# Retention and gMLP on one core: new order of SBUF slots, a later decay table, two weight sums by DMA

## The chip, the cores and the metric

The kernel runs on one core of one Trainium2 chip. The metric is device time in microseconds (us), from one launch to its end. Three runs of the kernel before are at hand; a fourth execution was recorded by the hardware profiler, and its span is the time from the first to the last instruction of the program.

## The reference

Two layers act on 512 latent tokens x and 256 context tokens ctx, 1024 wide, all in float32:

```python
h  = rmsnorm(x, g) * (1 + scale) + shift            # scale, shift, gate from c @ ada_w
# layer 0, bidirectional retention, 4 heads (q, k 256 wide; v, z 512 wide)
q, k, v, z = h @ w_in                                # q and k of latent tokens get axial rope
o  = sum over both directions of (q k^T * decay) v   # latent reads context + latent
x  = x + gate * ((o / rms(o)) * silu(z)) @ w_out
# layer 1, gMLP
u, v, z = h @ w_in                                   # each 2048 wide
v  = layernorm(v) * vnorm_g
y  = u * (w_s @ v + b_s) * silu(z)                   # w_s mixes 128 tokens, 8 groups
x  = x + gate * (y @ w_out)
return rmsnorm(x, final_g)
```

## The kernel before, in words

**Numbers in halves.** TensorE multiplies float32 operands in its fp32r form. So that the product keeps float32 accuracy, each operand is split in two: a high half, which ScalarE (ACT) makes by a cast, and a low half, which VectorE (DVE) makes as source minus high half (`split`, line 132). `mm3` (126) multiplies two operands by three matmuls: low by high, high by low, high by high. Each matmul first loads its stationary operand (128 columns, on the engine PEld of the profile) and then streams its moving operand (256 or 512 columns). The load for the next matmul runs while the present one streams.

**Products.** The matrices are cut in quarters, and a product of quarters by Strassen and Winograd's scheme takes seven products of sums in place of eight: B11, T1, T2, B21, T3, B22, T4 (`Product`, 435; `SINGLE`, 153; in pairs of weights `PAIRED`, 152). One such product is 24 matmuls of 256 columns. In `tokens` (425) the activations are stationary and the weights move; in `features` (396) and `outward` (415) the weights are stationary and the activations move. `WITH` (151) says which sum of activations (A11, A12, A22, S1 to S4) meets which sum of weights.

**Weights.** `Stream` (155) loads raw quarters into 4 KB slots (`pump`), makes the weights' sums T1 to T4 in place, and splits each into one of four `hl` slots (`upto`, two products ahead of use). T1 and T2 are sums on DVE (`sum`, 241). T3, and T4 of the weights `wo` and `o2`, are sums that the GpSimd queue (POOL) makes by an accumulating DMA from one raw slot onto another (`add`, 179; `by_queue`, 189).

**Order.** The order of the products is written out by hand. Within it, the framework's scheduler orders the instructions of each engine by readiness, save where a `Queue` (38) keeps or pins the order of the text; `bound` (1066) pins what it runs behind the instruction before it. The stages, with their place in the profile: layer 0's scores of modulation and first projection (to 56 us), the other projections (to 327), retention of heads 0 and 1 (`attend_two`, to 380), their output projection (`out_two`, to 419), head 2 (`attend_one`, 1344, and `project_out`, 1469, to 468), head 3 (to 522), gMLP's v (to 600), its u and z in eight quads `u` 0 to 7 (1898; to 820), with the output projection of the first half of y as the pair `o2` behind u 3 (`out_pair`, 1755; 685 to 725) and of the rest in `out1` (1782; from 788, and from 820 to the end).

**Retention.** `attend` (1244) makes scores for a pair of key blocks (`score`), on DVE multiplies them with the decay table into `pf`, splits them into `ph` (ACT) and `pl` (DVE), and two steps later multiplies them with v (`pv`, 512 columns). `decay` (1086) makes a head's tables by exponentials on ACT: first those of the latent keys, then those of the context keys (`ct`), then it loads Sqrt's table again. It is a generator: `plan` and `works` say behind which product its next piece is run. For head 2 all three pieces stand ahead of `attend_one` (1501 to 1503).

**gMLP.** For each quad u the normalized v is loaded into slot w7 (`load_vt`), normalized by four ACT instructions (`norm_vt`, 1857), and mixed by `spatial` in the middle of B22, the sixth product of the quad.

**Slots.** All of SBUF is laid out by hand: the `lay` lines (90 to 107) allot the slots one after another, each rounded up to 32 bytes. Counted modulo 256 bytes, the slots oA11 to oS4, hc, s1, w4, w5 and g3 begin at 0; s0, s2, s3, rope, w6, g2, w0 to w3, w7, g0, g1 and dec at 64; the t2 slots at 192. A weight in an `hl` slot begins at 64 where it is stationary and at 192 where it moves (`hl_tile`, 110). The first four weights of gMLP's v do not go there but into oS1, oS2, oA22 and oS3 (`hl_e`, 329 and 347), at 0. The operands `ye` of `o2` are two separate 4 KB halves (`halved_y`, 1712); the low half lies in g3 or s1 (at 0) for A11, S1, S4 and A22, and in s3 or g1 (at 64) for A12, S2 and S3.

```python
def hl_tile(moves=False):
    i = hls[0] % HL
    hls[0] += 1
    t = st([P, 2080], f"hl{i}", F32R, name="hl")
    o = 32 if moves != (i % 2 == 1) else 0
    return t[:, o:o + 2048].rearrange("p (a n) -> p a n", a=2)
```

Of the kernel before, what the change touches and what calls it, by code (L numbers as in the profile page):

```python
# [13 lines left out]
P = 128  # L14
# [53 lines left out]
def hybrid_kernel(ctx, tc, xT_d, cT_d, cv_d, sv_d, rows_d, ada0_d, adag_d, w_d, rope_d, dec_d, ws_d, id_d, out_d):  # L68
# [17 lines left out]
    HL = 4  # L86
# [7 lines left out]
    lay({"ones": 512, "sv": 448, "ident": 512, "eps": 4, "cpad": 1024, "root": 4, "lg": 32, "gs0": 64, "sh0": 64,  # L94
         "sq0": 16, "sq1": 16, "sq2": 16, "rs0": 1024, "rs1": 1024, "rs2": 1024, "shb": 16, "gate0": 32, "gs1": 32,
         "sh1": 32, "shs": 16, "la": 32, "lb": 32, "lc": 32, "sum0": 16, "sum1": 16, "bns": 256, "mv": 32, "rv": 16})
# [3 lines left out]
    lay({"oA11": 8192, "oA12": 8192, "oA22": 8192, "oS1": 8192, "oS2": 8192, "oS3": 8192, "oS4": 8192, "hc": 16384,  # L100
         "s1": 4096, "w4": 4096, "w5": 4096, "g3": 4096, "cv": 64})

    lay({"s0": 4096, "s2": 4096, "s3": 4096, "rope": 4096, "w6": 4096, "g2": 4096, "hl0": 8576})

    lay({"t2": 2048}, T2)
    lay({"hl1": 8320, "hl2": 8576, "hl3": 8320})
# [3 lines left out]
    def hl_tile(moves=False):  # L110

        i = hls[0] % HL
        hls[0] += 1
        t = st([P, 2080], f"hl{i}", F32R, name="hl")
        o = 32 if moves != (i % 2 == 1) else 0
        return t[:, o:o + 2048].rearrange("p (a n) -> p a n", a=2)
# [38 lines left out]
    class Stream:  # L155
# [23 lines left out]
        def add(self, must=None):  # L179

            for e in list(self.due):
                key, tick, to, src = e
                q = key[0]
                if (q, src) in self.raws and (key == must or self.tick > tick):
                    self.due.remove(e)
                    self.added.add(key)
                    nc.gpsimd.dma_start(self.raws[q, to], self.raws[q, src], accum_op=ALU.add)  # L187
# [53 lines left out]
        def sum(self, n):  # L241
# [17 lines left out]
            if name == "T2" and q[0] in ("wo", "o2"):  # L259
                self.due.append(((q, "T4"), self.tick, "21", "11"))  # L260
# [102 lines left out]
    for i in range(UZ):  # L363
# [3 lines left out]
        if i == 3:  # L367
# [3 lines left out]
            for u in ("11", "21", "12", "22"):  # L371
                for q in OUT1:
                    Q.load((q, u), W + ["w7"], 3, parts_of(q, u))
# [8 lines left out]
    def op(key):  # L382
        A[key] = st([P, 2, 4, HS], "o" + key, F32R)
# [378 lines left out]
    def come(*what, then=None):  # L762
# [3 lines left out]
        for kb, th in what:  # L766
# [4 lines left out]
            else:  # L771
                name = NAMES[th][g]
                if k == 0:
                    A[name] = st([P, 2, 4, HS], AT_S3.get(name, "o" + name), F32R)
# [311 lines left out]
    def decay(h, tags=None):  # L1086
# [60 lines left out]
    def load_wo(h):  # L1147
        raws = []
        for c in range(4):
# [5 lines left out]
            w = hl_tile()  # L1155
# [6 lines left out]
    def v_tile(h, tag):  # L1162

        if h != 1:
            return st([P, 2, 2, 512], tag, F32R, name="v")
        i = hls[0] % HL
        hls[0] += 1
        o = 16 if i % 2 else 48
        t = st([P, 2048 + o], f"hl{i}", F32R, name="v")
        return t[:, o:].rearrange("p (a b n) -> p a b n", a=2, b=2)  # L1170
# [173 lines left out]
    def attend_one(h, qs, vs, wo, steps, own=()):  # L1344

        og = [st([P, 2, 4, HS], tag, F32R, name="og") for tag in ("oS3", "oS4")]
# [9 lines left out]
        for i in range(2):  # L1356
            plan[i, 2] += [of(work) for work in own]
        return og, attend((h,), plan, turn)

    def attend_two(qs, vs, ds, q2):  # L1360
# [4 lines left out]
        def operand(key):  # L1365
            t = A[key] = st([P, 2, 4, HS], ROOM[key], F32R)
# [102 lines left out]
    def project_out(ws, og, flip, parts, then=None, between=None, prepare=None):  # L1469
        for hf in range(2):  # L1470
            sl = slice(hf * HS, hf * HS + HS)
            for c in range(4):
# [9 lines left out]
                for mi in range(2):  # L1482
# [25 lines left out]
    for work in own:  # L1508
        drained(work)
# [224 lines left out]
    def y_sums():  # L1734
        v = st([P, 4, HS], "g0", name="yv")
        dve.tensor_tensor(v, y22, y21, ALU.subtract)
        halved_y("S1", v, "g2", "g3")
# [9 lines left out]
        halved_y("S4", y12, "g2", "g3")  # L1747
# [4 lines left out]
        halved_y("A22", y22, "g2", "g3")  # L1752
        yield

    def out_pair():
# [3 lines left out]
        for name in PAIRED:  # L1759
            for q in OUT1:  # L1760
# [10 lines left out]
                n += 1  # L1771
        gb = Q.gate = st([P, D], "g1", name="gb")
        load(gb, gate_d.partition_broadcast(P))
        late_rows["fg"] = fg = st([P, D], "g0", name="fg")
        load(fg, rows_d[1:2, :].partition_broadcast(P))
        ya = st([P, 4, 2, SEQ], "hc", F32R, name="ya")
        ys.extend([ya[:, i] for i in range(4)] + [st([P, 2, SEQ], f"g{i}", F32R, name="yb") for i in (2, 3)])
# [120 lines left out]
    for i in range(UZ):  # L1898
        got, pms = {}, {}
        prod = Product(features, got.__setitem__)  # L1900
        for name in SINGLE:
# [5 lines left out]
            if name == "T2":  # L1907
                norm_vt(i)
# [4 lines left out]
            if name == "B22":  # L1913
# [5 lines left out]
                if i == 3:  # L1919
                    Q.free.append("w7")  # L1920
# [5 lines left out]
            if (i, name) == (2, "B21"):  # L1926
                halved_y("A11", y11, "s0", "s1")
# [3 lines left out]
        if i == 3:  # L1931
            out_pair()
            Q.free.remove("w7")
# [115 lines left out]
```

## Time and profile before

| | before |
|---|---|
| runs | 865.73, 863.9, 865.46 us; median 865.46 |
| profiled execution | 861.68 us |
| its span | 859.8 us (1.9 us lie around it) |
| granted TensorE clock in the span | 0.998 |
| busy in the span | PE 850.1, PEld 821.2, DVE 723.8, ACT 487.8, POOL 88.9 us |
| matmuls | 6966 |

A row of the timeline gives the start, the duration, the engine, the operation, output and inputs, and the count of instructions merged into it; the bracket behind it is the engine's idle time just before and what ended it. A matmul's duration reaches past the start of the next one, because matmuls are pipelined. The pitch, the time from one start to the next, is therefore taken between the starts of two rows, divided by the count. In a row of the groups by shape the columns behind the bar are busy time, mean duration of one in ns, and idle time before.

### The profile page before, as it was taken

To read this page: it belongs to the slowest core of one execution; us is meant where nothing else is said; L and a number is where in the kernel's file an instruction comes from. 1 tells how busy PE (TensorE), PEld (TensorE's weight loads), DVE (VectorE), ACT (ScalarE), POOL (GpSimd) and SP (SyncE) were. 2 spreads that over 40 slices of the span, in tenths; PEclk is the share of its full clock that TensorE was granted. 3 is DMA by queue.
4 is the path that set the end of the run, shared out by engine and by line. 5 is a ranking of instruction groups with operands and counts; after the bars stand their busy time and mean duration, and the time that the engine had idled before them with its cause. 6 is when DMAs were issued, how large, how long until landed. Compare 5 with 4: busy or idle time off the path is not lost.

```text
span 859.8 us, 17428 instructions
## 1 busy us (share of the span) xinstructions
PE 850.1 (99%) x6966; PEld 821.2 (96%) x6966; DVE 723.8 (84%) x1015; ACT 487.8 (57%) x770; POOL 88.9 (10%) x132
## 2 busy tenths in 40 slices
PE   9999999999999999999999999999999999999996
PEld 7899999999999999899989899999999999999985
DVE  4799899869977985799687879998888998788895
ACT  4566644455365355567873559754656665565434
POOL 0001211211211011000001012121000010000110
PEclk9999999999999999999999999999999999999999
DMA  9945857876977797257486943547555557546532
GB/s 358 406 131 154 245 175 255 261 216 183 311 218 226 221 305 264 75 123 219 162 273 186 261 113 111 197 135 244 173 148 144 152 129 215 154 141 197 123 49 99
DMA packets 82049, 166.70 MB, mean 194 GB/s; under 512 B 8624, under 2 KB 39728, under 8 KB 81968
## 3 DMA queue, kind: packets, MB, share of 16 engines
q1 hardware_dynamic: 68592, 122.90, 43.4%
q0 software_dynamic: 12944, 42.48, 20.1%
q8 instruction: 55, 0.90, 0.4%
q10 hardware_dynamic: 432, 0.20, 0.1%
q14 instruction: 26, 0.21, 0.1%
HBM read 125.17 MB, written 24.12 MB: 174 GB/s over the span
## 4 chain that ended last, share of the span: by engine, by line
PE 94%; ACT 3%; DMA 1%; DVE 1%; issue 1%; ACTq 0%; DVEq 0%
PE pst L54 94%; DMA vt<-vt 1%; DMA ident<-in_id_dram 1%; ACT acc L54 0%; DVE o L54 0%; ACT L54 0%; ACT junk L54 0%; ACT hl L54 0%; ACT dt L54 0%; ACT vt L54 0%; ACT qk L54 0%; DVE snap L54 0%; ACT de L54 0%; DVE ada_h L54 0%; DVE v L54 0%
## 5 line engine op out<-in xcount | busy, mean ns | idle before, releaser
L54 DVE TENSOR_TENSOR hl<-raw,hl 128x1024 fp32r<-128x1024 f32 (+2 forms) x209 | 249.7, 1200 | 56.4 <-ACT hl L54 55.9
L54 ACT CAST hl<-raw 128x1024 fp32r<-128x1024 f32 (+2 forms) x209 | 214.4, 1031 | 128.6 <-DVE raw L54 61.9
L54 PE MATMUL pst<-oS,hl 128*128 128x256 f32 x1296 | 155.2, 277 | 0.1
L54 PEld LDWEIGHTS pst<-oS,hl 128*128 128x128 f32 x1296 | 150.6, 188 | 1.2 <-issue 0.8
L54 PE MATMUL pst<-hl,oS 128*128 128x256 f32 x1152 | 134.7, 276 | 0.0
L54 PE MATMUL pst<-oA,hl 128*128 128x256 f32 x1080 | 133.9, 279 | 0.1
L54 PEld LDWEIGHTS pst<-hl,oS 128*128 128x128 f32 x1152 | 132.4, 188 | 0.8 <-issue 0.4
L54 PEld LDWEIGHTS pst<-oA,hl 128*128 128x128 f32 x1080 | 127.3, 188 | 1.8 <-issue 0.4
L54 DVE TENSOR_TENSOR raw<-raw 128x1024 f32<-128x1024 f32 x77 | 93.9, 1220 | 0.9
L54 PE MATMUL pst<-hl,oA 128*128 128x256 f32 x768 | 92.1, 277 | 0.0
L54 ACT ACTIVATE snap<-pst 128x512 f32<-128x512 f32 x87 | 51.7, 594 | 68.0 <-PE pst L54 67.9
L54 PEld LDWEIGHTS pst<-hl,oA 128*128 128x128 f32 x768 | 89.3, 188 | 0.0
L54 PE MATMUL pst<-v,ph 128*128 128x512 f32 x192 | 59.8, 393 | 0.0
L187 POOL DMA_DIRECT2D raw<-raw x31 | 27.0, 870 | 278.8 <-DVE raw L54 166.9
L54 DVE TENSOR_TENSOR snap<-snap,pst 128x512 f32<-128x512 f32 x75 | 51.0, 680 | 3.0 <-PE pst L54 2.9
L54 PE MATMUL pst<-og,hl 128*128 128x256 f32 x384 | 46.3, 280 | 0.0
L54 PEld LDWEIGHTS pst<-og,hl 128*128 128x128 f32 x384 | 45.0, 188 | 0.2
L54 PEld LDWEIGHTS pst<-v,ph 128*128 128x128 f32 x192 | 36.1, 188 | 7.0
L54 PE MATMUL pst<-hl,ye 128*128 128x256 f32 x336 | 40.4, 282 | 0.0
L54 PEld LDWEIGHTS pst<-hl,ye 128*128 128x128 f32 x336 | 40.1, 188 | 0.1
L54 PE MATMUL pst<-v,pl 128*128 128x512 f32 x96 | 37.8, 394 | 0.9 <-DVE pl L54 0.9
L54 ACT CAST ph<-pf 128x512 fp32r<-128x512 f32 x24 | 14.9, 621 | 40.2 <-DVE pf L54 40.2
(240 smaller groups left out, 1134.9 us busy)
## 6 DMA issues: line engine op xcount, KB each, us to landing
raw<-in_w_dram SPq DMA_DIRECT2D x208, 256.0 KB, 3.9
bg<-in_adag_dram SPq DMA_DIRECT2D x32, 512.0 KB, 5.1
raw<-raw POOLq DMA_DIRECT2D x31, 512.0 KB, 5.4
ada_w<-in_ada_dram SPq DMA_DIRECT2D x16, 512.0 KB, 8.5
raw<-in_w_dram SPq DMA_DIRECT2D x16, 512.0 KB, 4.5
v<-snap POOLq DMA_DIRECT2D x16, 256.0 KB, 4.6
z<-snap POOLq DMA_DIRECT2D x16, 256.0 KB, 4.5
v<-v SPq DMA_DIRECT2D x8, 512.0 KB, 6.7
```

Of the source, the lines that this page charges most:

```text
L54: made = op(*args, **kw)
L187: nc.gpsimd.dma_start(self.raws[q, to], self.raws[q, src], accum_op=ALU.add)
```

## The change

**Slots.** The `lay` lines are put in another order, and the slots oA22, oS1, oS2 and oS3 get 64 bytes more. Their operands (`big`) begin 64 bytes into the slot. `hl_part` replaces `hl_tile`'s two cases by a wanted residue: `STATIONARY` 0, `MOVING` 128 and `SHIFTED` -64, counted from the first `hl` slot. Modulo 256 the slots oA22, oS1, oS2 and oS3 now begin at 192, and their operands at 0; the first `hl` slot begins at 64, so that stationary weights lie at 64, moving ones at 192 and shifted ones at 0. All other operands of matmuls keep their residues, but for these: `hl_e` lies at 192; the weights of `o2` are shifted, at 0; the output weights of head 3 and of quad u 6 are stationary but lie at 192; the second weights of `out1`'s parts 9 and 11 lie at 128; the low halves `ye` that lay in g3 or s1 lie in w7 or g1, at 64; and the `yb` of `out1` that lay in g3 (at 0) lie in g0 (at 64).

**Swapped slots.** g3 takes the place of w7 as the eighth raw slot of `o2`, and holds the final norm's row `fg`; w7 holds low halves of `ye` up to the end of `o2`.

**Two sums.** T2 of the two `o2` weights is made by an accumulating DMA of the POOL queue, issued behind the split of T1, where DVE made it; T4's DMA comes due behind it.

**Decay and halves of head 2.** The context's table is made behind the first scores in `attend_one`, and Sqrt's table is loaded two steps later. The pieces that load and halve v stand about one product earlier.

**`norm_vt`** is pinned behind T2's own instructions.

```diff
@@ Stream.add, by_queue
                     nc.gpsimd.dma_start(self.raws[q, to], self.raws[q, src], accum_op=ALU.add)
+                    if key[1] == "T2":
+                        self.due.append(((q, "T4"), self.tick, "21", "11"))
-            return name == "T3" or (name == "T4" and q[0] in ("wo", "o2"))
+            return name == "T3" or (name == "T4" and q[0] in ("wo", "o2")) or (name == "T2" and q[0] == "o2")
+        def home(self, q):
+            if q[0] == "o2":
+                return SHIFTED
+            if q[0] == "o":
+                return -SHIFTED if q[1] in (9, 11) else STATIONARY
+            return MOVING if q[0] in ("vz", "v", "z", "v1") or q == ("u", 6) else STATIONARY
@@ Stream.upto
-                hl = place() if place else hl_tile(q[0] in ("vz", "v", "z", "v1", "o2"))
+                hl = place() if place else hl_tile(self.home(q))
...
+                if name == "T1" and self.by_queue(q, "T2"):
+                    self.due.append(((q, "T2"), self.tick, "11", "22"))
@@ layout
+    def big(shape, tag, name=None):
+        o = AHEAD // 4 if tag in ("oA22", "oS1", "oS2", "oS3") else 0
+        t = st([P, 2048 + o], tag, F32R, name=name)[:, o:]
+        return t.rearrange("p (a b c) -> p a b c", a=shape[1], b=shape[2])
+    STATIONARY, MOVING, SHIFTED = 0, 128, -64
+    def hl_part(to, name):
+        i = hls[0] % HL
+        hls[0] += 1
+        t = st([P, HL_SIZE // 4], f"hl{i}", F32R, name=name)
+        o = (to - i * HL_SIZE) % 256 // 4
+        return t[:, o:o + 2048]
@@ decay
+        if h == 2:
+            yield
         act.activation(root, eps, AF.Sqrt)
@@ load_wo
-            w = hl_tile()
+            w = hl_tile(MOVING if h == 3 else STATIONARY)
@@ attend_one, out_two
-        for i in range(2):
-            plan[i, 2] += [of(work) for work in own]
+        for i, works in enumerate(own):
+            plan[i, 2] += [of(work) for work in works]
...
-    out_two(flip, {1: (ss,), 2: (ss,), 3: (ds,), 4: (ss,), 6: (vs,), 7: (ss,), 8: (vs, qs, ds), 9: (qs,), 10: (vs, vs, qs),
-                   11: (qs, ds, wo2), 12: (vs,)})
-    drained(ds)
-    own = (vs, qs)
+    out_two(flip, {1: (ss,), 2: (ss,), 3: (ds,), 4: (ss,), 6: (vs,), 7: (ss,), 8: (vs, qs, ds), 9: (qs, vs), 10: (vs, qs),
+                   11: (qs, vs, wo2)})
+    own = (ds, vs), (qs, vs), (qs, ds)
@@ gMLP
-        halved_y("S1", v, "g2", "g3")
+        halved_y("S1", v, "g2", "w7")
...
-                norm_vt(i)
+                bound(lambda: norm_vt(i))
...
-                halved_y("A11", y11, "s0", "s1")
+                halved_y("A11", y11, "s0", "g1")
```

More of the change, by code (lines that the diff above doesn't have):

```diff
@@ L258, in sum @@
                 self.due.append(((q, "T3"), self.tick, "12", "22"))
-            if name == "T2" and q[0] in ("wo", "o2"):
+            if name == "T2" and q[0] == "wo":
                 self.due.append(((q, "T4"), self.tick, "21", "11"))
@@ L372, in hybrid_kernel @@
                 for q in OUT1:
-                    Q.load((q, u), W + ["w7"], 3, parts_of(q, u))
+                    Q.load((q, u), W + ["g3"], 3, parts_of(q, u))
         if i == UZ - 2:
@@ L1164, in v_tile @@
         if h != 1:
[L1165 to L1170, printed above, removed]
+            return big([P, 2, 2, 512], tag, "v")
+        return hl_part(SHIFTED, "v").rearrange("p (a b n) -> p a b n", a=2, b=2)
     def load_v(h):
@@ L1344, in attend_one @@
     def attend_one(h, qs, vs, wo, steps, own=()):
-        og = [st([P, 2, 4, HS], tag, F32R, name="og") for tag in ("oS3", "oS4")]
+        og = [big([P, 2, 4, HS], tag, "og") for tag in ("oS3", "oS4")]
         def turn(h, hf, flipped):
@@ L1507, in hybrid_kernel @@
     og, flip = attend_one(2, qs, vs, wo2, {5: 1, 6: 1}, own)
-    for work in own:
-        drained(work)
     project_out(wos.pop(2), og, flip, (decay(3), vs, qs))
@@ L1751, in y_sums @@
         yield
-        halved_y("A22", y22, "g2", "g3")
+        halved_y("A22", y22, "g2", "w7")
         yield
@@ L1771, in out_pair @@
                 n += 1
+        Q.free.remove("g3")
         gb = Q.gate = st([P, D], "g1", name="gb")
         load(gb, gate_d.partition_broadcast(P))
-        late_rows["fg"] = fg = st([P, D], "g0", name="fg")
+        late_rows["fg"] = fg = st([P, D], "g3", name="fg")
         load(fg, rows_d[1:2, :].partition_broadcast(P))
         ya = st([P, 4, 2, SEQ], "hc", F32R, name="ya")
-        ys.extend([ya[:, i] for i in range(4)] + [st([P, 2, SEQ], f"g{i}", F32R, name="yb") for i in (2, 3)])
+        ys.extend([ya[:, i] for i in range(4)] + [st([P, 2, SEQ], tag, F32R, name="yb") for tag in ("g0", "g2")])
     def yf(f):
@@ L1919, in hybrid_kernel @@
                 if i == 3:
-                    Q.free.append("w7")
+                    Q.free.append("g3")
                     Q.pump()
@@ L1932, in hybrid_kernel @@
             out_pair()
-            Q.free.remove("w7")
             load_vt(4)
```

32 lines of the change are left out of this document (16 added, 16 removed).

## The prediction

> **What bounds the kernel now.** I read the page first, then TensorE's waits, then the groups by shape, then the timeline of TensorE stage by stage.
>
> ```profile
> span 859.8 us, 17428 instructions
> PE 850.1 (99%) x6966; PEld 821.2 (96%) x6966; DVE 723.8 (84%) x1015; ACT 487.8 (57%) x770; POOL 88.9 (10%) x132
> PE 94%; ACT 3%; DMA 1%; DVE 1%; issue 1%; ACTq 0%; DVEq 0%
> ```
> ```profile
> PE pst L54 <- DVE eps L54: 1.1, 1, 1.1
> PE pst L54 <- DVE pl L54: 0.9, 1, 0.9
> PE pst L54 <- DMA ident<-in_id_dram: 0.8, 1, 0.8
> ```
>
> TensorE is busy all the time and its waits sum to 2.8 us. So time can come only from the pitch of its matmuls, from the one wait on `pl`, and from stalls too short for the list. The pitch is not the same everywhere. I call d the address where the next weight load starts, minus the address where the running matmul's moving operand starts, modulo 256 bytes (the change's words count it the other way round). With the residues of the slots, d is 64 for nearly all matmuls of 256 columns, 0 where `hl_e` moves, 128 for the high halves `ye` (two loads of three).
>
> ```profile
> L54 PE MATMUL pst<-hl,oS 128*128 128x256 f32 x1152 | 134.7, 276 | 0.0
> L54 PE MATMUL pst<-hl,ye 128*128 128x256 f32 x336 | 40.4, 282 | 0.0
> L54 PE MATMUL pst<-hl_e,oA 128*128 128x256 f32 x96 | 12.4, 285 | 0.0
> ```
> ```profile
> 413.43 5.60 PE L54 MATMUL pst<-oA,hl 128*128 128x256 f32 x48
> 418.87 4.24 PE L54 MATMUL pst<-qk 128*128 128x256 f32 x36
> ...
> 521.81 3.04 PE L54 MATMUL pst<-hl_e,oA 128*128 128x256 f32 x24
> 524.69 1.03 PE L54 MATMUL pst<-ident,acc 128*128 128x128 f32 x8
> ...
> 688.93 36.71 PE L54 MATMUL pst<-hl,ye 128*128 128x256 f32 x306
> 725.47 2.89 PE L54 MATMUL pst<-oA,hl 128*128 128x256 f32 x24
> ```
>
> From start to start: (418.87 - 413.43)/48 = 113.3 ns at d = 64; (524.69 - 521.81)/24 = 120.0 ns at d = 0; (725.47 - 688.93)/306 = 119.4 ns for `ye`. Durations go the same way (276, 285, 282 ns). Distance is not everything, though: the same d = 64 also runs at a second pitch.
>
> ```profile
> 666.53 5.79 PE L54 MATMUL pst<-oS,hl 128*128 128x256 f32 x48
> 672.16 2.99 PE L54 MATMUL pst<-oA,hl 128*128 128x256 f32 x24
> 674.98 5.11 PE L54 MATMUL pst<-oS,hl 128*128 128x256 f32 x42
> ...
> 505.40 4.49 PE L54 MATMUL pst<-og,hl 128*128 128x256 f32 x36
> 509.72 1.03 PE L54 MATMUL pst<-ident,acc 128*128 128x128 f32 x8
> ```
>
> (674.98 - 672.16)/24 = 117.5 ns, 4.2 more than 113.3, in operands that run at 113.3 in other quads; head 3's output projection shows 4.32/36 = 120.0 ns with a step out of transposes in it. TensorE seems to fall into this slow pitch at a stall and to keep it until another break. Both kinds of loss are what the change can win.
>
> **The change part by part.** *Weights of `o2`.* d becomes 64 for all 336 matmuls. For the 306 of the row above that is 306 x 6.1 ns = **1.9 us** gained; the 30 ahead of them are left out, because an inserted fp32 matmul and the change of pattern stand there. The condition is that DVE keeps up:
>
> ```profile
> 685.00:697.00 12.00, 12.00 (x104) 12.00 (x103) 12.00 (x17) 7.44 (x9) 1.68 (x2) 1.00 0.51 107
> 697.00:711.00 14.00, 14.00 (x119) 13.92 (x119) 14.00 (x14) 10.04 (x12) 0.84 (x1) 1.00 0.63 159
> ```
> ```profile
> 700.85 1.22 DVE L54 TENSOR_TENSOR raw<-raw 128x1024 f32<-128x1024 f32 x1
> ```
> ```profile
> L187 POOL DMA_DIRECT2D raw<-raw x31: 832/862/938, 61.3 to 789.8; - x31
> ...
> DMA to landing us min/median/max: 4.4/5.4/7.5
> ```
>
> In these windows the columns are TensorE, PEld, DVE, ACT, POOL: DVE is full for all 26 us. A TensorE that is 5% faster takes 1.2 us from these 26; the two T2 sums, 1.22 us each by the row, give 2.4 back. So the transfers do not gain by themselves; they pay for the pitch. Their own cost is time to land, 4.4 to 7.5 us. T1's split can start when its `hl` slot comes free, five products (5 x 24 x 113.3 ns = 13.6 us) ahead of T2's matmuls. I estimate 3 us for it (a cast, a subtraction and their queues) and 2.3 us for T2's own split behind the landing: 8.3 us are free, against 7.5 at worst. What queues behind it: on POOL T3's and T4's transfers, needed four products or more later; on ACT and DVE the casts of the next weights. I take nothing, bounds 0 to 2 us lost. The Trainium skill (SBUF — State Buffer, "Who interferes with whom") says that a DVE instruction with two SBUF inputs blocks a GpSimd instruction that reads SBUF; POOL's 832 to 938 ns for all 31 show no such block here.
>
> *`hl_e`.* 96 matmuls from 120.0 to 113.3: **0.6 us**.
>
> *Head 3's output projection* gets d = 192. For 256 columns no long stretch here has it; the nearest rows are 113.3 at d = 64 and 120.0 at d = 0. I take 113.3, since what is lost there is the slow pitch: 144 matmuls behind the first insertion x 4.2 ns = **0.6 us**; bounds -0.7 (120 for all 192, against about 117) to +0.6. Quad u 6, likewise moved, runs at 113.3 now: 0, bounds -1.1 (168 x 6.7 ns) to 0.
>
> ```profile
> 788.10 1.54 PE L54 MATMUL pst<-hl,ya 128*128 128x512 f32 x6
> 789.47 1.56 PE L54 MATMUL pst<-hl,yb 128*128 128x512 f32 x6
> 790.87 1.53 PE L54 MATMUL pst<-hl,ya 128*128 128x512 f32 x6
> ```
>
> *512 columns.* 1.37/6 = 228 ns for `ya` (d = 192), 1.40/6 = 233 for `yb`, which mixes 0 and 192 and gets 192: 48 x 5 ns = **0.2 us**.
>
> *Context's decay of head 2.*
>
> ```profile
> 417.08 0.83 ACT L54 ACTIVATE dt<-exps,lg 128x640 f32<-128x640 f32 x1
> 417.81 1.00 ACT L54 ACTIVATE de<-exps,lg 128x512 f32<-128x512 f32 x2
> 418.83 1.28 ACT L54 ACT_TABLE_LOAD   x1
> 420.12 0.20 ACT L54 ACTIVATE root<-eps 128x1 f32<-128x1 f32 x1
> 422.60 0.64 ACT L54 CAST ph<-pf 128x512 fp32r<-128x512 f32 x1
> 424.02 0.50 PE L54 MATMUL pst<-v,pl 128*128 128x512 f32 x1 [0.91 <-DVE pl L54]
> ...
> 426.21 0.69 DVE L54 TENSOR_TENSOR pl<-pf,ph 128x512 fp32r<-128x512 f32 x1
> ...
> 428.25 0.39 PE L54 MATMUL pst<-v,pl 128*128 128x512 f32 x1
> ```
>
> TensorE is through its 36 score matmuls at 418.87 + 36 x 0.1133 = 422.95 and starts on `pl` at 424.02: **1.1 us** lost, because ACT reaches the first cast `ph` only at 422.60. 3.3 us of ACT's work (the first four rows) leave its place ahead of `ph`, so the cast comes in time. They come back behind it, with 0.9 us of additions on DVE, ahead of the second `pl`: that one ends at 426.90 and is needed at 428.25, 427.2 once TensorE starts earlier. So 0 to 0.6 us may return; I take 0. Halves of v that move a product forward stand beside matmuls that never wait.
>
> *`norm_vt` pinned.*
>
> ```profile
> 645.64 2.08 ACT L54 ACTIVATE vt<-vt,nm,rv 128x256 f32<-128x256 f32 x4 [1.78 <-DMA vt<-vt]
> 647.62 0.58 ACT L54 ACTIVATE snap<-pst 128x512 f32<-128x512 f32 x1
> 648.25 2.81 PEld L54 LDWEIGHTS pst<-oS,hl 128*128 128x128 f32 x24 [0.29 <-ACT snap L54]
> ```
>
> ACT waits for the load of v, normalizes for 2.08 us, and only then drains a bank that T2 must reuse: 0.3 us in u 2, with its restart 0.4. In u 3 the same happens, and TensorE keeps the slow pitch from there to the end of the quad (the rows at 672.16 and 674.98): five products x 24 x 4.2 ns = 0.5. Together **0.9 us**. Pinned behind T2, the 2.1 us lie beside three products (8.2 us) ahead of their use in B22. For u 4, v's load now waits for w7, so until `o2` is over; its use comes five products (13.6 us) later, and load and normalization need less than 8. Cost 0; if the load also holds back raw quarters queued behind it on SP, a wait like the longest behind the start, 0.9 us.
>
> *The rest.* g3 for w7 as raw slot frees a load from waiting on v: 0.
>
> Sum: 1.9 + 0.6 + 0.6 + 0.2 + 1.1 + 0.9 = **5.3 us**. The profiled execution took 861.68 us, 3.8 below the median of the runs, so I take the difference alone: 865.46 - 5.3 = **860.2 us**.
>
> **The rivals.** *Addresses do nothing.* The Trainium skill speaks for it: by the page and section named above, TensorE reads moving operand and weights through two independent ports and never waits on anyone; d could not matter. As a mechanism of this kernel: the pitch would belong to the order of matmuls (which a stall sets), and `o2`, `hl_e` and head 3 stay where they are. For it: two pitches at one d. Against it: the stretches at d = 0 and 128 are slow throughout, while the 1152 matmuls of the first row by shape, at d = 64, average 276 ns; the trace so far disagrees with two free ports. Left are 1.1 + 0.9 = 2.0 us: **863.5 us**.
>
> *The slow pitch spreads* (slower than before). Every start in the stages behind head 2 shifts. If TensorE met its break at the wrong moment in all eight quads u (8 x 7 x 24 = 1344 matmuls) and in `out_two` (336), 1680 x 4.2 ns = 7.1 us would be lost: 865.46 - 5.3 + 7.1 = **867.3 us**. It decides from (5.3 + 1.7)/0.0042 = 1670 matmuls on. For it: u 3 kept the slow pitch for five products. Against it: the insertions of `spatial` break every quad, and the other quads come out fast.
>
> *T2 lands late.* If POOL takes T4's transfer of the first weight ahead of T2's of the second, that T2 waits for one more landing, and casts queue on ACT and DVE, which is full: 2 us back, **862.2 us**.
>
> **How the numbers follow.** As planned, 860.2: 0.66. Addresses do nothing, 863.5: 0.15. T2 late, 862.2: 0.12. Slow pitch spread, 867.3: 0.07. A measurement can tell 0.2%, 1.7 us, from no change: the bound is 863.7. The first and third case are faster; the second lies just inside, so a third of it is counted as no change, and of the fourth 0.05 as slower and 0.02 as no change. So faster 0.88 by count; I take 0.04 off for unknown sizes: 0.84, same 0.11, slower 0.05. The range goes down by the 1.6 us by which the lowest run before lies under the median, and 0.6 us for slow stretches that may break elsewhere (to 858.0), and up over the two cases behind to 864.2.
>
> **What would show it.** Right: `ye` and `hl_e` at mean durations near 276 ns; the 306 matmuls of `o2` in about 34.7 us; no row of waits on `pl`; no PEld gap by `snap` in u 2 and u 3; DVE under 26 us in the first 25 of `o2`. Wrong: `ye` still near 119 ns (addresses do nothing); rows of u at 117.5 ns where they are 113.3 now (slow pitch); TensorE idle in the T2 products of `o2` (late landing).

## The result and the profile after

| | before | after |
|---|---|---|
| runs, median (lowest to highest) | 863.76 us (861.41 to 865.73) | 867.45 us (865.47 to 872.13) |
| after / before | | 1.0051, 95% interval 1.0038 to 1.0063 |
| profiled execution, its span | 861.68, 859.8 us | 868.53, 866.8 us |

Each median is of 20 runs. The change makes the kernel 0.5% slower: 3.7 us lost where 5.3 were forecast as won. The profiled execution shows more, 7.0 us of span.

TensorE's groups by shape and its waits, in after:

```profile
L54 PE MATMUL pst<-hl,ye 128*128 128x256 f32 x336 | 41.3, 286 | 2.8 <-ACT hl L54 2.0 <-DVE hl L54 0.9
L54 PE MATMUL pst<-hl_e,oA 128*128 128x256 f32 x96 | 12.0, 282 | 0.0
```
```profile
PE pst L54 <- ACT hl L54: 2.0, 1, 2.0
...
PE pst L54 <- DVE qk L54: 0.9, 1, 0.9
PE pst L54 <- DVE hl L54: 0.9, 1, 0.9
```

The wait on `pl` is gone. A new wait on the halves `qk` has its size, and two waits on `hl` are new: both stand in `o2`, whose `ye` matmuls went to 286 ns each, not to 276. The timeline of TensorE there:

```profile
688.83 15.90 PE L54 MATMUL pst<-hl,ye 128*128 128x256 f32 x138
706.68 0.38 PE L54 MATMUL pst<-hl,ye 128*128 128x256 f32 x1 [1.95 <-ACT hl L54]
707.94 21.46 PE L54 MATMUL pst<-hl,ye 128*128 128x256 f32 x167 [0.87 <-DVE hl L54]
729.24 2.99 PE L54 MATMUL pst<-oA,hl 128*128 128x256 f32 x24
732.06 4.17 PE L54 MATMUL pst<-oS,hl 128*128 128x256 f32 x34
```

Up to the stall TensorE is early: 138 matmuls in 15.90 us, so (15.90 - 0.28)/137 = 114.0 ns each with an inserted fp32 step in them, 113.3 without. Then it stands still ahead of the first two matmuls of T2's second product, from 704.45 to 707.94 us: 3.5 us from start to start (stalls are given so from here on), 3.3 over the normal pitch. And behind `o2` u 4 does not run at 113.3 ns as it did before, but at (732.06 - 729.24)/24 = 117.5, and so does all up to the end of u 7. The difference to before is 0.1 us ahead at 688.8, 3.8 behind at the first row of u 4 (729.24 against 725.47), and 6.6 at the last matmul. So all of it is lost from 704 us on. What did TensorE wait for? DVE, POOL and ACT in the same stretch:

```profile
693.01 1.22 DVE L54 TENSOR_TENSOR raw<-raw 128x1024 f32<-128x1024 f32 x1
...
697.15 1.22 DVE L54 TENSOR_TENSOR hl<-raw,hl 128x1024 fp32r<-128x1024 f32 x1
```
```profile
696.91 0.84 POOL L200 DMA_DIRECT2D raw<-raw  x1 [1.32 <-DMA raw<-raw]
698.66 0.85 POOL L200 DMA_DIRECT2D raw<-raw  x1 [0.90 <-DVE hl L54]
```
```profile
705.58 1.04 ACT L54 CAST hl<-raw 128x1024 fp32r<-128x1024 f32 x1 [4.72 <-DMA raw<-raw]
```

DVE makes T1's sum of the second weight at 693.01 and comes to its low half only at 697.15. The transfer of T2's second sum, which overwrites what that low half reads, is issued at 698.66, behind T4's transfer of the first weight (696.91). ACT's cast waits for the landing until 705.58: 6.9 us. And the windows of the stall and of what follows (TensorE, PEld, DVE, ACT, POOL, granted clock, DMA share, GB/s):

```profile
704.00:708.00 4.00, 1.18 (x9) 0.78 (x7) 1.34 (x2) 2.42 (x4) 0.85 (x1) 1.00 0.90 284
708.00:712.00 4.00, 4.00 (x22) 4.00 (x23) 4.00 (x4) 3.38 (x5) 0.00 (x0) 0.61 0.57 113
```

Behind the stall the granted clock is 0.61 in the mean of 4 us: 22 matmuls, where 35 fit at 113.3 ns. That loses another 1.5 us in these 4 us and about 1.9 until the clock is back. By the starts of the single matmuls the pitch right behind the stall is back at 113 to 116 ns (708.29 to 708.86); then each matmul takes 213 ns until 712.2, and 118 ns from there on. So three losses stand in a row: a stall, a low clock, a slow pitch, and here the slow pitch begins where the clock comes back. The runs below take them apart.

At head 2, DVE in after:

```profile
423.79 0.89 DVE L54 TENSOR_TENSOR dt<-dt,de 128x512 f32<-128x512 f32 x2
425.03 1.23 DVE L54 TENSOR_TENSOR v<-v 128x1024 fp32r<-128x1024 f32 x1 [0.34 <-ACT v L54]
426.17 0.69 DVE L54 TENSOR_TENSOR pl<-pf,ph 128x512 fp32r<-128x512 f32 x1
426.77 0.69 DVE L54 TENSOR_TENSOR qk<-qk 128x512 fp32r<-128x512 f32 x1
```

The additions to the context's table and a half of v now stand ahead of the second q's low half; TensorE, through with `pv` at 426.3, waits for it until 427.5.

### The profile page after: what moved, and what is told of

Its sections match the earlier page's. It is cut to its first block, busy times and chain, and to the rows that moved or that the text cites. A ratio compares the mean times of both kernels' runs of the same rounds, so it can differ in the third digit from the quotient of the medians.

```text
span 866.8 us, 17432 instructions
## 1 busy us (share of the span) xinstructions
PE 853.0 (98%) x6966; PEld 822.6 (95%) x6966; DVE 720.7 (83%) x1013; ACT 487.8 (56%) x770; POOL 90.7 (10%) x134
## 4 chain that ended last, share of the span: by engine, by line
PE 89%; DMA 5%; DVE 3%; ACT 1%; issue 1%; SPq 0%; DVEq 0%; ACTq 0%
PE pst L54 89%; DMA ada_w<-in_ada_dram 2%; DMA cq<-in_cT_dram 1%; DMA raw<-raw 1%; DVE hl L54 1%; DMA cv<-in_cv_dram 0%; DVE o L54 0%; DVE ya L54 0%; DMA raw<-in_w_dram 0%; SPq L54 0%; DVE yv L54 0%; DVE raw L54 0%; ACT hl L54 0%; ACT junk L54 0%; DVE snap L54 0%
## 5 line engine op out<-in xcount | busy, mean ns | idle before, releaser
L54 DVE TENSOR_TENSOR raw<-raw 128x1024 f32<-128x1024 f32 x75 | 91.3, 1218 | 0.6
L54 PEld LDWEIGHTS pst<-qk 128*128 128x128 f32 x288 | 35.6, 188 | 2.3 <-DVE qk L54 1.2
```

What stands on the lines that cost most here:

```text
L54: made = op(*args, **kw)
```

## The experiments

Ratios are to the kernel before, timed on the same chip in the same rounds, with the 95% interval (e11 and e12 have 5 runs, e5 has 11, the others 12).

| run | median us | ratio to before |
|---|---|---|
| e1 T2 on DVE | 863.05 | 1.0001 (0.9992 to 1.0009) |
| e2 T2's transfer alone | 864.27 | 1.0020 (1.0006 to 1.0033) |
| e3 T4 behind T2 | 862.40 | 0.9994 (0.9982 to 1.0006) |
| e4 halves ahead of decay | 864.50 | 1.0017 (1.0005 to 1.0029) |
| e5 u 6, head 3 at 64 | 862.29 | 1.0001 (0.9990 to 1.0012) |
| e6 o2 at 128 | 864.10 | 1.0014 (1.0003 to 1.0025) |
| e7 T1 sooner | 863.86 | 1.0011 (1.0000 to 1.0021) |
| e8 all mended | 862.45 | 0.9990 (0.9978 to 1.0002) |
| e9 yb back | 862.93 | 0.9988 (0.9973 to 1.0003) |
| e10 second T2 on DVE | 862.21 | 0.9992 (0.9982 to 1.0003) |
| e11 wash-out | 860.33 | 0.9960 (0.9944 to 0.9976) |
| e12 combined | 860.03 | 0.9962 (0.9948 to 0.9976) |
| e13 after, washed | 865.90 | 1.0027 (1.0014 to 1.0040) |
| e14 combined, no T2 transfer | 861.71 | 0.9980 (0.9968 to 0.9992) |
| e15 low half first | 859.59 | 0.9956 (0.9942 to 0.9970) |
| e16 v washed | 861.14 | 0.9975 (0.9963 to 0.9988) |

### The late sum: e1, e2, e3

**e1**, on after:

```diff
-            return name == "T3" or (name == "T4" and q[0] in ("wo", "o2")) or (name == "T2" and q[0] == "o2")
+            return name == "T3" or (name == "T4" and q[0] in ("wo", "o2"))
...
-            if name == "T2" and q[0] == "wo":
+            if name == "T2" and q[0] in ("wo", "o2"):
```


> The kernel after, but T2 of the two o2 weights is summed on DVE again, as before the change; slots, decay and norm_vt stay changed. Theory A (one late sum): the landing of T2's second transfer at 705.6 us stops TensorE for 3.3 us, the granted clock then drops to 0.61 for 4.4 us (1.9 us lost), and TensorE keeps a pitch of 117.8 ns in place of 113.3 from there to the end of u 7 (792 matmuls x 4.5 ns = 3.6 us, and some more in 512-column products). Without that transfer all three go: 867.5 - 3.3 - 1.9 - 3.3 = about 859 us, 4 to 5 us under the kernel before, and all quads u 4 to u 7 at 113.3 ns. Theory B (the new addresses bring the slow pitch in u 4 to u 7): the stall and the low clock go, the 117.8 ns stay: about 862.3 us. Theory C (a full DVE stalls the faster TensorE in o2): stalls of 1 us or more come back in o2 at other places, 861 to 866 us.

The low clock and the slow pitch of u 4 to u 6 are gone, but a stall stays: 1.7 us in T2's second product, now on DVE (the row of waits: `DVE hl`, 1.4 us). Theory A holds for what follows the stall; theory C holds too: DVE is too full for the faster TensorE. Result 863.05, no change to before and 4 us above theory A's 859: neither place for T2 is good as it stands.

**e2**: before, with T2's sums of `o2` by transfers and T4's behind them, as in after.

> The kernel before, with one part of the change: T2 of the two o2 weights by transfers on POOL; slots and all else as before. Theory A: TensorE reaches the second T2 product about 0.9 us later than in the kernel after (119 ns pitch), so it stalls 2 to 3 us, the clock drops behind that, and u 4 to u 7, which run at 113.3 ns in the kernel before, take 117.8 ns: 863.8 + 2.4 + 1.9 + 3.3 = about 871 us, if the clock and the slow pitch follow a stall of 2.4 us as they follow one of 3.3. Theory B: the stall and perhaps the low clock come, u 4 to u 7 stay at 113.3 ns: 866 to 868 us. If T2's transfer lands in time here, no change: 863.8 us.

The last case came nearest: T2 lands in time, since DVE's order there lets the second transfer go at 693.92, not at 698.66. A stall of 1.1 us comes later instead (719.0, on DVE), with no low clock, and u 4 runs at 113.3 ns. 1.2 us slower.

**e3**, on after, with the POOL queue pinned for `o2`:

```diff
-                        self.due.append(((q, "T4"), self.tick, "21", "11"))
+                        self.due.append(((q, "T4"), self.tick + 1, "21", "11"))
...
+                    self.pool.pinned = q[0] == "o2"
```


> The kernel after, with one order changed on POOL: T4's transfer of the first o2 weight is issued behind T2's of the second, not ahead of it. Theory A with contention (T4's transfer, in flight at the same time, is what makes T2's take 6.9 us): T2 lands about 1.5 us sooner, the stall shrinks to 1 to 2 us; if so short a stall lets clock and pitch alone, 861 us, if not, 866 us. Theory A without contention (T1's split on DVE, which ends at 698.4, is what makes it late): landing, stall and time stay, 867.5 us.

POOL, ACT and TensorE:

```profile
698.47 1.72 POOL L54 DMA_DIRECT2D raw<-raw  x2 [3.07 <-DVE hl L54]
```
```profile
703.37 1.05 ACT L54 CAST hl<-raw 128x1024 fp32r<-128x1024 f32 x1 [2.71 <-DMA raw<-raw]
```
```profile
688.63 16.23 PE L54 MATMUL pst<-hl,ye 128*128 128x256 f32 x139
705.74 19.22 PE L54 MATMUL pst<-hl,ye 128*128 128x256 f32 x167 [0.88 <-DVE hl L54]
724.79 2.88 PE L54 MATMUL pst<-oA,hl 128*128 128x256 f32 x24
727.51 5.60 PE L54 MATMUL pst<-oS,hl 128*128 128x256 f32 x48
```

The transfer is issued 0.2 us sooner than in after and lands in 4.9 us, not 6.9, with T4's behind it. The stall falls to 1.3 us, the clock stays at 1.00, u 4 to u 6 run at 113.3 ns, and the ratio falls from 1.0051 to 0.9994: 0.57%, 4.9 us, for the order of one pair of transfers. That is more than the whole loss of 3.7 us.

### The addresses: e6, and the wait at head 2: e4

**e6**, on e3 (one constant):

```diff
             if q[0] == "o2":
-                return SHIFTED
+                return MOVING
```


> The kernel with T4's transfer behind T2's (862.4 us), and the weights of o2 at 192 in place of 0, so that the next load of a low or high half starts 128 bytes from the moving operand (d = 128 in place of 64) and nothing else moves. Theory (the distance sets the pitch): the products of o2 take 117.5 to 119 ns again where they take 113.3, 336 x 5 ns = 1.7 us, of which 0.7 to 0.9 come back because TensorE reaches the late T2 product so much later (a stall of 0.4 to 0.6 in place of 1.26 us): 863.3 us. Rival (addresses do nothing; the pitch comes with the order of work): o2 stays at 113.3 ns and 862.4 us.

```profile
706.26 20.09 PE L54 MATMUL pst<-hl,ye 128*128 128x256 f32 x167 [0.16 <-DVE hl L54]
726.18 2.89 PE L54 MATMUL pst<-oA,hl 128*128 128x256 f32 x24
```

The last 167 matmuls take (726.18 - 706.26)/167 = 119.3 ns at d = 128, against (724.79 - 705.74)/167 = 114.1 at d = 64 in e3. The order is the same and one address differs, so the distance sets the pitch; the stall shrinks as expected, to 0.4 us. By the ratios e6 is 0.20% above e3, 1.7 us, where 0.9 were expected; the intervals just overlap. The Trainium skill (SBUF — State Buffer, "Who interferes with whom") gives TensorE independent read ports for moving operand and weights and has it never wait on anyone; by that the address should not matter, and these runs disagree by 5 ns for each matmul.

**e4**, on after:

```diff
-    own = (ds, vs), (qs, vs), (qs, ds)
+    own = (qs, vs), (ds, vs), (qs, ds)
```


> The kernel after, with one order changed in head 2: the piece that halves the second q goes ahead of the piece that makes the context's decay, not behind it. If the 1.2 us that TensorE waits at 426.3 us for those halves come from DVE's additions to the decay table and a half of v ahead of them, the wait goes: 867.5 - 1.1 = 866.4 us. Rival: the wait moves to the next probabilities, whose low half or decay table now is late: 867.5 us and a wait on pl or on the context's scores near 429 us.

```profile
425.89 1.53 PE L54 MATMUL pst<-qk 128*128 128x256 f32 x12
427.26 0.39 PE L54 MATMUL pst<-v,pl 128*128 128x512 f32 x1
```

No wait is left there, and none comes behind it: 1.2 us won at this place. The run as a whole is 0.34% under after, more than this edit explains; in its profile `o2` stalls by 3.7 us and the clock falls to 0.5 as in after, but u 4 to u 6 run at 113.3 ns. So the slow pitch does not follow from the stall each time.

### The slow pitch: e5, e9, e13, e11, e16

**e5**, on e3: u 6 and head 3 back at d = 64.

```diff
-            return MOVING if q[0] in ("vz", "v", "z", "v1") or q == ("u", 6) else STATIONARY
+            return MOVING if q[0] in ("vz", "v", "z", "v1") else STATIONARY
...
-            w = hl_tile(MOVING if h == 3 else STATIONARY)
+            w = hl_tile()
```


> The kernel with T4's transfer behind T2's (the run before, 862.4 us), and with the weights of quad u 6 and of head 3's output projection back at 64, as every other stationary weight (d = 64 in place of 192). Theory (an insertion of fp32 matmuls at d = 192 leaves TensorE in the slow pitch of 117.8 ns, at d = 64 it comes back to 113.3): the last product of u 6 and all seven of u 7 run at 113.3 in place of 117.8 (192 x 4.5 ns = 0.9 us with what follows in 512 columns), head 3's first 48 matmuls at 114 in place of 117.7 (0.2 us): 862.4 - 1.0 = 861.4 us. Rival (the slow pitch of u 7 comes from elsewhere, the raised speed of what lies ahead of it): u 7 stays at 117.8, 862.2 to 862.4 us.

Head 3 and `hl_e`, first in after, then in e5:

```profile
496.08 5.81 PE L54 MATMUL pst<-og,hl 128*128 128x256 f32 x48
501.73 1.03 PE L54 MATMUL pst<-ident,gt 128*128 128x128 f32 x8
...
522.78 2.99 PE L54 MATMUL pst<-hl_e,oA 128*128 128x256 f32 x24
525.61 1.04 PE L54 MATMUL pst<-ident,acc 128*128 128x128 f32 x8
```
```profile
496.11 5.62 PE L54 MATMUL pst<-og,hl 128*128 128x256 f32 x48
501.57 1.03 PE L54 MATMUL pst<-ident,gt 128*128 128x128 f32 x8
...
522.46 2.90 PE L54 MATMUL pst<-hl_e,oA 128*128 128x256 f32 x24
525.20 1.04 PE L54 MATMUL pst<-ident,acc 128*128 128x128 f32 x8
```

At d = 192 head 3 is slow from its first matmul (117.7 ns; 113.8 at 64) and hands the slow pitch on to the first product of `hl_e` (117.9; 114.2). From its first matmul to `hl_e` head 3 takes 26.70 us in after and 26.35 in e5, so d = 192 loses 0.35 us. All of `hl_e`, to the start of the next product, takes 12.92 us in both: what e5 wins in the first product it loses in the second. The last product of u 6 runs at 113.9 ns, where it took 117.8 in e3. For u 7 the theory fell: it starts at 117.5 ns here too.

```profile
798.56 2.99 PE L54 MATMUL pst<-oA,hl 128*128 128x256 f32 x24
801.38 4.88 PE L54 MATMUL pst<-oS,hl 128*128 128x256 f32 x40
```

**e9**, on e5: the old slots of `out1`.

```diff
-        late_rows["fg"] = fg = st([P, D], "g3", name="fg")
+        late_rows["fg"] = fg = st([P, D], "g0", name="fg")
...
-        ys.extend([ya[:, i] for i in range(4)] + [st([P, 2, SEQ], tag, F32R, name="yb") for tag in ("g0", "g2")])
+        ys.extend([ya[:, i] for i in range(4)] + [st([P, 2, SEQ], tag, F32R, name="yb") for tag in ("g2", "g3")])
...
-                return -SHIFTED if q[1] in (9, 11) else STATIONARY
+                return STATIONARY
```


> The run with u 6 and head 3 at 64 (862.3 us), and of the slots swapped for out1 the old ones: yb in g2 and g3, fg in g0, the second weights of parts 9 and 11 at 64. Its yb products of 512 columns then have d = 0 and 192 mixed again. Theory (the new slots of yb leave TensorE in the slow pitch behind the first products of out1): all seven products of u 7 and the last 256-column products of the kernel run at 113.3 ns in place of 117.8, 192 x 4.5 ns = 0.9 us less, and nothing for 512 columns: 861.4 us. Rival (the slow pitch of u 7 has another cause): u 7 stays at 117.8 ns, 862.3 us.

```profile
798.21 2.91 PE L54 MATMUL pst<-oA,hl 128*128 128x256 f32 x24
800.96 5.26 PE L54 MATMUL pst<-oS,hl 128*128 128x256 f32 x45
```

(800.96 - 798.21)/24 = 114.6 ns, and 113.3 for the rest of u 7: the slots of the 48 matmuls of 512 columns ahead of it decide how u 7 runs. With the old slots it is fast in every profile (before, e2, e9, e12, e14 to e16), with the new ones it is slow in all but e11 and e13, whose first product of u 7 is at another distance. The gain, 0.8 us, is in the rows; the runs (860.3 to 865.5) scatter too much to show it.

**e13**, on after: a stretch at d = 128 behind the stall ("wash-out").

```diff
+            if q[0] == "o2" and name == "T4":
+                return MOVING
+            if (q, name) == (("u", 7), "B11"):
+                return -SHIFTED
```


> The kernel after, with one thing changed: T4's two products of o2 and the first of u 7 at d = 128 (72 matmuls, 0.4 us). Theory: stall (3.3 us) and low clock (1.9 us) in o2 stay, the slow pitch that they set ends at T4's products: u 4 to u 6 at 113.3 ns (2.2 us where the state had lasted) and u 7 too (0.65 us): 867.5 - 2.2 - 0.65 + 0.4 = 865.0 us, with runs closer together than the 865.5 to 872.1 of the kernel after. Rival (stall and low clock set the state anew, or most runs of the kernel after had no slow pitch in u 4 to u 6): 866.5 to 867.5 us.

By the ratios 0.24% under after: 2.1 us, where 2.5 were expected. In its profile the stall set no slow pitch, so for u 4 to u 6 the stretch had nothing to end. In u 7 it had: the last product of u 6 takes 117.8 ns a matmul, the first of u 7, at d = 128, (805.08 - 802.20)/24 = 120.0, and the rest (810.52 - 805.08)/48 = 113.3.

```profile
802.20 3.04 PE L54 MATMUL pst<-oA,hl 128*128 128x256 f32 x24
805.08 5.61 PE L54 MATMUL pst<-oS,hl 128*128 128x256 f32 x48
810.52 2.88 PE L54 MATMUL pst<-oA,hl 128*128 128x256 f32 x24
```

The profile also shows something of the clock; the windows, with the same stall as in after (3.5 us from 705.59):

```profile
704.00:708.00 4.00, 2.05 (x18) 1.85 (x16) 0.91 (x2) 1.29 (x2) 0.85 (x1) 1.00 0.95 237
708.00:712.00 4.00, 3.13 (x26) 2.93 (x26) 4.00 (x4) 4.00 (x6) 0.00 (x0) 1.00 0.91 220
```

Here the clock stays at 1.00. The same stall lowered it in after and e4; stalls of 1.1 to 1.7 us did not in the profiles of e1, e2 and e3. Over all executions, the mean granted clock of the span is 0.996 or less in 22 of the 44 of after, e4 and e13, and in 4 of the 153 of the other runs of the table. The Trainium skill (TensorE: Matmul & The Clock Gate, Part 1) says that the clock falls to half behind an idle window of about 3.4 us, and that the windows run freely, so that phase matters. The profiles agree on the length: the clock is at 0.50 for 3.4 us in after (708.9 to 712.3) and for 6.8 us in e4 (704.9 to 711.8). But the time ahead of the fall was not idle throughout: in those 3.4 us TensorE was busy for 1.3 us in after and for 1.4 us in e4. So 3.5 us of stall can lower the clock and need not, and 1.7 us did not.

**e11**, on e8 (which is e3 with e4, e5 and e7 together; u 4 to u 7 ran at 117.8 ns in its profile): the same wash-out.

> All four mends on the kernel after: T4's transfer behind T2's, T1's halves sooner, the halves of head 2's second q ahead of the decay, weights of u 6 and head 3 at 64. If the causes are separate and add up: 862.4 - 1.1 - 1.1 - 1.0 = 859.2 us, 0.4% under the kernel before. If something else sets the end, less of it arrives; TensorE's rows then show at which stage.

> The run with all four mends (862.4 us), in which o2 kept a stall of 0.8 us and u 4 to u 7 ran at 117.8 ns in the profile, and now T4's two products of o2 and the first product of u 7 get weights at another residue, so that d is 128 in these 72 matmuls alone (5 ns more for each, 0.4 us). Theory (the slow pitch is a state that a stall sets and that a stretch at another distance ends, as the 336 matmuls of o2 at d = 128 do in the kernel before): u 4 to u 6 and six products of u 7 at 113.3 ns whatever the stall does: 862.4 - 2.2 - 0.65 + 0.4 = 860.0 us. Rival (the state follows the stall alone): u 4 to u 7 as in that run, 117.8 ns, 862.8 us.

e8 got 862.45, not 859.2: a stall of 0.8 us stays in T2, and from a gap of 0.3 us in the last product of `o2` on, all runs at 117.8 ns. With 72 matmuls at another distance e11 is at 860.33 as expected, 0.3% below e8.

**e16**, on e15 below: a stretch at d = 128 in gMLP's v.

```diff
+            if (q, name) == (("v1", 2), "B11"):
+                return -SHIFTED
```


> The kernel with the low halves in order (859.6 us), and the first weight of the second half of gMLP's v at 128 in place of 192, so that 24 matmuls have d = 128. In the profile of the kernel without this, v runs at 117.8 ns from 556 to 600 us. Theory (a stretch at d = 128 ends the slow pitch in any form of product): the rest of v, 13 products, at 113.3 ns in every run, 13 x 24 x 4.5 ns = 1.4 us less in the runs that had the slow pitch and 0.1 us more in the others: median 858.9 us, and the runs in one group under 860.5. Rival (the slow pitch is chance, and nothing that 24 matmuls do ends it): 859.6 us and two groups as before.

This profile refutes the wash-out as a rule. Two cuts of its timeline, ahead of the 24 matmuls and behind them:

```profile
558.36 3.11 PE L54 MATMUL pst<-hl,oA 128*128 128x256 f32 x26
```
```profile
564.04 3.23 PE L54 MATMUL pst<-hl,oA 128*128 128x256 f32 x26
```

With 0.28 us for the last matmul of a cut, v runs at 2.83/25 = 113.2 ns ahead of the stretch and at 2.95/25 = 118.0 behind it: the change of distance put TensorE *into* the slow pitch. The run is 1.5 us above e15. A change of distance sets the pitch anew; what decides into which of the two is not shown.

### DVE's order: e7, e10, e12, e14, e15

**e7**, on e3: `w = Q.get(3 if n == 2 else 2)` in `out_pair`, so T1's halves come one product sooner.

> The kernel with T4's transfer behind T2's (862.4 us), and the halves of o2's second T1 one product sooner, ahead of a 1.2 us addition on DVE. Theory (T2's transfer is late because T1's low half, which must be read first, queues on the full DVE): the transfer is issued about 1.4 us sooner, lands near 702 us, and the stall of 1.26 us in T2's second product falls to 0.3 or less: 862.4 - 1.1 = 861.3 us. Rival (DVE is full, so the 1.2 us come back one product later at the low half of the activations' sum, which waits behind): a stall of about 1 us at the first T2 product, 862.4 us.

The transfer goes 1.5 us sooner (696.95) but takes 6.0 us to land, perhaps because T3's, issued 2.4 us ahead, is still in flight: the stall only falls to 1.0 us, and in the profile it sets the slow pitch up to u 7. The ratio is above e3's (1.0011 against 0.9994), but the intervals overlap.

**e10**, on e5: `by_queue` takes T2 for `("o2", 0)` alone; DVE sums the second.

> The run with u 6 and head 3 at 64 (862.3 us), but only the first o2 weight's T2 by a transfer, the second's by a sum on DVE. Theory (the stall of 1.7 us in T2's second product is the landing of a transfer that shares the DMA engines with two others; with both sums on DVE it was DVE that was late): with one sum DVE has the 1.2 us, since it stood idle for 1.1 us on that landing; the stall falls from 1.7 to 0.4 us or less, 861.0 us. Rival (DVE has no room for even one sum): a stall of 1 to 1.7 us stays, 862.3 us or more.

A stall of 1.3 us stays (1.7 in the profile of e5). DVE shows why:

```profile
701.62 1.22 DVE L54 TENSOR_TENSOR raw<-raw 128x1024 f32<-128x1024 f32 x1
...
703.89 2.35 DVE L54 TENSOR_TENSOR hl<-raw,hl 128x1024 fp32r<-128x1024 f32 x2
```

Of the two low halves in the last row, the first is that of B22, which TensorE needs a product later; T2's ends at 706.2, needed at 705.0.

**e12**: e5 with e4, e9, e10 and T4's products of `o2` at d = 128.

> Everything that pays by the theories together: the kernel after with T4's transfer behind T2's, one T2 on DVE, halves of head 2's second q ahead of the decay, u 6 and head 3 at 64, yb in g2 and g3, T4's products of o2 at d = 128. Theory: no stall over 0.4 us in o2, no wait at 426 us, u 4 to u 7 at 113.3 ns: 863.0 (before) - 1.9 + 0.2 (o2) - 0.6 (hl_e) - 1.1 (pl) - 0.9 (norm_vt) + 0.4 = 859.1 us, 0.45% under the kernel before. Rival (the time comes back elsewhere): 860.5 to 862.5 us.

The stall of 1.3 us remains and sets the slow pitch; the median, 860.03, lies between the theory and the rival. T4's products end the slow pitch, and u 4 starts at 113.8 ns:

```profile
704.65 19.98 PE L54 MATMUL pst<-hl,ye 128*128 128x256 f32 x167 [1.05 <-DVE hl L54]
724.47 2.89 PE L54 MATMUL pst<-oA,hl 128*128 128x256 f32 x24
727.20 5.60 PE L54 MATMUL pst<-oS,hl 128*128 128x256 f32 x48
```

**e14**: e12 with both T2 on DVE.

> The combined kernel (860.0 us) with both T2 sums of o2 on DVE. Theory (DVE is full for 26 us, so one sum more puts 1.2 us on TensorE): the stalls in o2 grow from 1.3 to 2.0 us or more, as in the first run (0.35 + 1.67 us): 860.8 us. Rival (DVE's order and not its load makes the stall, the transfer is worth nothing): 860.0 us.

Stalls of 0.3, 0.3 and 1.8 us and 861.71 us: by the ratios the one transfer left in e12 is worth about 1.6 us, though the two intervals overlap a little.

**e15**: e12, with the halves of `o2`'s first B22 pinned behind those of the second T2.

```diff
+                if (q, name) == (("o2", 0), "B22"):
+                    bound(lambda: split((hl[:, 0, :], hl[:, 1, :]), r))
```


> The combined kernel (860.0 us), and on ACT and DVE the halves of o2's first B22 pinned behind those of the second T2, which TensorE needs a product earlier. Theory (the 1.3 us that are left are this order: the 1.2 us of B22's low half stand ahead of T2's): the stall falls to 0.3 us or less, 859.0 us. Rival (DVE's load): the wait moves to B22's product, 860.0 us.

```profile
688.85 35.66 PE L54 MATMUL pst<-hl,ye 128*128 128x256 f32 x306
724.35 2.91 PE L54 MATMUL pst<-oA,hl 128*128 128x256 f32 x24
```

The 306 matmuls run without a gap that the list shows, (724.35 - 688.85)/306 = 116.0 ns with 48 of them at d = 128, against 119.4 before. At 859.59 us and 0.44% under before this is the lowest median; e11 and e12 lie within its interval, so its lead on them is not shown. Its runs still scatter from 858.4 to 862.4 us. Its profile shows v at 117.8 ns from 556 to 600 us, which costs 1.8 us in that execution; whether the faster runs lack it was not shown.

## Why the prediction was wrong

**The step that failed** is T2's transfer: "I estimate 3 us for it (a cast, a subtraction and their queues)", "8.3 us are free", "I take nothing, bounds 0 to 2 us lost". T1's split was done 7.4 us after its slot came free (691.0, 18 matmuls behind the row at 688.83, to 698.4), not 3, on an engine that the prediction itself shows as full. The 3 us left out that DVE must make T1's sum first (693.01 to 694.23); ACT's cast follows to 695.36, and the low half waits for DVE until 697.15. With 0.3 us to the issue, 6.9 to the landing and 2.3 for T2's split that makes 16.9 us where 13.6 were free: 3.3 too late, what the trace shows. The trace of before could have shown how much was free. There DVE ends T2's second low half at 705.5:

```profile
703.12 2.36 DVE L54 TENSOR_TENSOR hl<-raw,hl 128x1024 fp32r<-128x1024 f32 x2
```

TensorE came to that product at 705.4, by the starts in the trace, and to its second matmul at 705.5. So nothing was free at all, and a sum of 1.2 us was replaced by 6.9 us of transfer in front of a TensorE made faster.

**A second step failed with it**: "the transfers do not gain by themselves; they pay for the pitch". The transfer makes the kernel slower (e1 and e3 show it), but without it the forecast 5.3 us do not arrive either: e1, with the sums on DVE, is at 1.0001. By the starts in its profile it loses 2.0 us in `o2`, 1.1 on the second q, 0.4 in head 3 and 0.9 in u 7 and the end. Where most of these were mended and one sum was left on POOL, 0.38% (e12) and 0.44% (e15) were won, 3.3 and 3.8 us. The absolute forecast also stood on a base, 865.46 us from three runs, that was 1.7 us above the median of the twenty.

**The rival "T2 lands late"** had the mechanism right, T4's transfer ahead of T2's included, and the size wrong: 2 us, where e3 shows 4.9. It priced the wait, not what a wait leaves behind: a low clock in some executions and the slow pitch in some. "The slow pitch spreads" gave 867.3 us, near the result, but not by its mechanism: of its stages only u 4 to u 7 took the slow pitch, as a sequel of this stall with its low clock and of the slots of `out1`; `out_two` and u 0 to u 3 did not.

**By the other terms.** `o2`'s pitch: right, 113.3 ns at d = 64 (e6 isolates it), but the gain of 1.9 us was eaten by the stall. `norm_vt`: right, though no run takes the pinning alone. The gap in u 2 is gone, u 3 keeps 113.3 ns, where before had 117.5, and between 640 and 685 us after gains 0.9 us on before, as forecast:

```profile
672.57 2.88 PE L54 MATMUL pst<-oA,hl 128*128 128x256 f32 x24
675.29 4.92 PE L54 MATMUL pst<-oS,hl 128*128 128x256 f32 x42
```

Context's decay: 1.1 forecast, about 0 got; the prediction looked at the second `pl` as the next to be late, and it was the second q (e4). `hl_e`: 0.6 forecast, 0.2 got (13.13 us before, 12.92 in after). The pitch at its first 24 matmuls was carried over to all 96, of which the other 72 stand among inserted fp32 steps; head 3's slow pitch is not the reason, since e5 takes 12.92 us too. Head 3: 0.6 forecast, 0.3 lost (26.37 us before, 26.70 in after); the value taken for d = 192 was wrong at a start behind fp32 matmuls. 512 columns: 0.2 forecast, none got, and u 7 with the end lost 0.8 (e9). u 6: 0 taken, 0.1 lost in its last product (e5). v's late load in u 4: 0, as taken. The retention of heads 0 and 1 lost 0.3 us between 352 and 380 us, where 256 columns took 113 ns before and take 118 in after; the prediction has no term for it, and its cause is open.

## What to carry to other kernels

Before a sum is moved from a full engine to a transfer, measure in the trace how long before its use the sum ends now; if that is nothing, the transfer's landing and whatever is in flight beside it go straight onto the path. Price a stall on a busy TensorE with what it leaves behind: the clock, and the pitch of the matmuls that follow. Where two operands' addresses are brought to the faster distance everywhere, look also for the changes of distance that were lost, since such a change can end a slow state or begin one.

## What the runs showed of the hardware

- Matmuls of 256 columns at one distance (d = 64) have two pitches, 113.3 and 117.8 ns, and keep either for 100 us and more (after, 712 us to the end of u 7), through insertions of fp32 matmuls. A stall can set the slow one (1.0 us in e7, 1.3 in e12, a gap of 0.3 in e8) or not (1.3 us in e3, 3.7 in e4, 3.5 in e13); in after it begins where the low clock ends. A change of distance sets one or the other: behind `o2` with d = 128 at its end, u 4 ran fast in every profile here (before, e2, e6, e11 to e16); in v it ran slow (e16). What decides it stays open.
- An accumulating transfer of 512 KB issued 1.75 us behind another took 6.9 us to land (after); with the other one issued behind it, 4.9 us (e3), one execution each.
- After stalls of 3.5 to 3.7 us the granted clock fell to half in two of three profiles (after, e4; not e13), for 3.4 and 6.8 us, and the pitch was 213 ns there.
